# Sparse attention scores with a full-height rest of the keys, and block values in two 64-column products

## The chip, the cores and the metric

The program runs on one core of a Trainium2 chip, as one launch. The metric is the device time of one execution, in microseconds (us). TensorE multiplies matrices, VectorE and ScalarE work element by element, GpSimd (POOL) does some of that too, and SyncE (SP) issues most transfers between memory and the on-chip SBUF. TensorE writes only to PSUM, which is handed out here as two-bank tiles (`p2`, three of them) and one-bank tiles (`p1`, two of them).

## The reference, cut to what matters

Two transformer blocks on 512 tokens of 1024 features, in float32. The second block has two layers, each a mixer and a mixture of 16 experts. The mixer of its second layer is a sparse attention (`nsa_mixer`) with 16 heads of 64 features in 4 groups; the four heads of a group share keys and values. Each query is matched with three sets of keys, each with a softmax of its own, and the three results are added under gates:

```
p_cmp = masked_softmax(einsum('bghqd,bgcd->bghqc', qb, k_cmp), cmask)   # 31 compressed blocks
o_cmp = einsum('bghqc,bgcd->bghqd', p_cmp, v_cmp)
...                                                                     # the 16 best blocks of 64 keys
o_slc = einsum('bghqk,bgqkd->bghqd', p_slc, v_sel)
...                                                                     # the last 512 keys
o_win = einsum('bghqk,bgkd->bghqd', p_win, vw_b)
o = gb[..., 0:1] * o_cmp + gb[..., 1:2] * o_slc + gb[..., 2:3] * o_win
```

With 512 tokens there are 8 blocks, fewer than 16, and the window holds 512 keys, so both the selected and the window branch reach every earlier key under a causal mask. They differ in their keys and values.

## The kernel before, in words

Products that must be exact are done in rounded parts. A float32 matrix is split into a part rounded to the type `float32r` and the rest, and a product is the sum of rounded by rounded, rounded by rest and rest by rounded (`mm3`, L393 to L396, three matmuls into the same PSUM tile). Values and weights of the attention that stay plain float32 take two TensorE instructions for a product.

The attention works on token tiles of 128 queries, from the last tile (number 3) to the first, because the last sees the most keys: tile i sees n = 128(i+1) of them. Its steps, with their lines:

- `k_turn` (L1717) turns the keys of both branches feature-major, four token tiles one by one. The 64 features of each group stand twice, on rows 0 to 63 and 64 to 127. ScalarE rounds them into `kH` (L1725, two pages of SBUF, one for two groups); VectorE subtracts to get the rest into `kL` (L1728), one page: even groups on rows 0 to 63, odd groups on rows 64 to 127, so two subtractions of 64 rows for each pair of groups.
- The compressed keys `ck` (L1783 to L1790) hold the rounded part on all rows and beside it the rest, on the rows that meet the queries' rounded part, else zero. They have a small tile of their own. The compressed values `vbd` (L1797) are block-diagonal: for each group and each pair of heads a stationary matrix of 128 rows (4 heads of 32 block slots) by 128 columns (2 heads of 64 features).
- `q_parts` and `q_turn` (L1806, L1819) make the stacked queries `qT`: for a head, its rounded part on 64 rows and its rest on the other 64; which is on top depends on the group's parity.
- `weights` (L1869) does the scores of a head: for each branch one matmul of the stacked queries with `kH` (L1880, 128 rows, so both the rounded and the rest part of the queries), one of the queries' rounded part with `kL` (L1881, 64 rows), and one that adds the causal mask in bfloat16 (L1882, 128 columns). In the first two tiles, where 2n is at most 512, both branches go in one matmul each and two heads share a PSUM tile. VectorE then takes the row maximum (L1885), ScalarE the exponentials with their sums (L1889), VectorE scales by gate over sum (L1890 to L1894).
- `turn` (L1897) turns the weights with n/128 matmuls a branch and head (L1905), ScalarE copies them to SBUF (L1907).
- `values` (L1910) does a pair of heads: one product of `vbd` with the compressed weights, both heads at once (L1912, 128 columns, two instructions), then for each branch, key tile and head a product of 64 columns (L1916, two instructions each), the first head into rows 0 to 63 of the PSUM tile and the second into rows 64 to 127.

`csc` (L1836) and `compressed` (L1849) do the scores and weights on the compressed keys. The loop of L1942 runs over (tile, head); the scores run two heads ahead of the turns. When tile 1 begins, the output projection of tiles 2 and 3 (`project`, L1209) is mixed in three steps at a time, its matmuls being L394 to L396 with the name `op`. Behind the attention follow the projection of tiles 0 and 1, the routing, 16 experts and the last layer norm.

Two things set the order of work. The program is written in one order, and a planner with a simulated timeline (`schedule_with_timeline_sim`) then fixes each engine's instruction order at build time. And SBUF is handed out in 23 pages of four units by the class `Arena` (L209): `take` gives a request that needs a whole page the page that was freed longest ago, and `float32r` values and plain ones do not share a page. A tile on a reused page waits for the last reader of what was there. `kH0`, `kH1`, `kL` take three pages and are followed by the rounded and rest parts of the weights of the first key projection (`wh`, `wl`, L376).

Of the kernel before, what the change touches and what calls it, by code (L numbers as in the profile page):

```python
# [10 lines left out]
F32 = mybir.dt.float32  # L11
# [31 lines left out]
# ------------------------------------------------------------------ host side layout  # L43
# [164 lines left out]
# ------------------------------------------------------------------ device side  # L208
class Arena:  # L209
    """SBUF in pages of four units, handed out and taken back in the order of the program.  # L210

    A page holds either rounded values or plain ones; a free page that changes sides becomes a new tile."""
# [56 lines left out]
def build(ctx, tc, I, out, dbg=None):  # L269
# [36 lines left out]
    def load_a(name, dt=F32):  # L306
        """a constant in the arena, to be dropped after its last use"""
        ap = I[name]
        t = sb(ap.shape[1], name, dt)[:ap.shape[0]]
        nc.sync.dma_start(out=t, in_=ap)  # L310
        return t

    def after(i, name):
        """let an instruction go behind one that is needed sooner"""
        tc.add_manual_dep(i.ins, name, mybir.DependencyInfo(mybir.DependencyClass.NoSync, mybir.DependencyReason.SCHED_ONLY),
                          reason="what is needed sooner goes first")

    class Stream:
        """Weights in the order of their use, a page at a time; the ring's depth sets how far the loads run ahead."""
# [8 lines left out]
        def ahead(self, n):  # L328
            """request the next n pages here"""
# [11 lines left out]
        def later(self, ld):  # L341
            """queue a load behind those that are needed sooner"""
# [55 lines left out]
    def dense_fm(nk, x, cols, alloc=p2):  # L398
        """one 128-row output tile; x(k, sl) -> (H, L); cols: list of slices"""
# [7 lines left out]
    def tiles(n, w, tag, dt=F32):  # L407
        """n tiles of w columns, as many to a page as fit"""
# [17 lines left out]
    def newton(dst, xh, t):  # L426
        """a step towards 1/sqrt of one value per partition, of which xh holds minus a half, in two"""
# [5 lines left out]
    def rsq(dst, src, shape):  # L433
        """1/sqrt of a small positive tile, by Newton's steps from a guess on the bits"""
# [7 lines left out]
    # ---------------------------------------------------------------- load and split x  # L442
# [26 lines left out]
    def rstd_wide(dst, ps, cols, n):  # L469
        """1/sqrt(sum/n + eps) on every partition"""  # L470
# [17 lines left out]
    # ---------------------------------------------------------------- ssm: the transition and its powers  # L488
# [16 lines left out]
    def sincos(x, mul, nm):  # L505
        """sin and cos of mul*x, the argument brought to [-pi, pi]"""
# [20 lines left out]
    def cmul(ore, oim, ar_, ai, br, bi, ta, tb, eng, neg_im=False, conj=False):  # L527
        """(a)(b); conj: conj(a) b; neg_im: minus the imaginary part"""
# [56 lines left out]
    def big_cmul(o, fs, m0, xr, xi, neg_im, eng):  # L585
        """[pair, m, c] = lb^(m0+m) * x[pair, c]"""
# [40 lines left out]
    # rotation of the chunks' states  # L627
# [89 lines left out]
    # queries and gates fill the waits of the ssm; the gates are kept in memory until the mixing  # L717
# [45 lines left out]
    # ---------------------------------------------------------------- keys and values  # L763
# [52 lines left out]
    # ---------------------------------------------------------------- attention  # L816
# [21 lines left out]
    def att_out(osb, ss4, n, t0, skip=0):  # L838
        """sub-layer norm of n tokens of all heads, then transposed into the mixed tokens at t0"""
# [57 lines left out]
    # the mixer's own tail fills the waits of the attention  # L897
# [16 lines left out]
    def gated(m, ps):  # L914
        """(tanh + 1) * y, twice the sigmoid's product"""
# [71 lines left out]
    # ---------------------------------------------------------------- mixing, residual  # L987
# [34 lines left out]
    # ---------------------------------------------------------------- ffn  # L1022
# [25 lines left out]
    # ================================================================ second block  # L1048
# [14 lines left out]
    # the router's weights under the first layer norm of each layer: gain into the rows, the sums for mean and bias  # L1063
# [17 lines left out]
    # ---------------------------------------------------------------- gla in  # L1081
# [40 lines left out]
    def stream_tm(x, mid=None):  # L1122
        """token-major product, the weights streamed once; four [128, 512] accumulators; mid() goes in between"""
# [32 lines left out]
    # ---------------------------------------------------------------- layer norm, output projection, experts  # L1156
# [6 lines left out]
    def stats(bs, rs, mv):  # L1163
        """per token: 1/sqrt(var + eps), -mean/sqrt(var + eps), and the mean; of the sum over alpha; an operation a step"""
# [19 lines left out]
    def run(steps, n=None):  # L1184
        """the next n steps, or the rest of them"""
# [5 lines left out]
    class Layer:  # L1191
# [11 lines left out]
        def clear(self):  # L1203
            """rows of slots that no token takes"""
# [4 lines left out]
        def project(self, pair, free=()):  # L1209
            """two token tiles, in steps: the output projection, the weights streamed once for both, then the routing"""  # L1210
# [4 lines left out]
            def scores(nh):  # L1215
                """what half the features add to the router's scores"""
# [72 lines left out]
        def taken(self, pos, k, t):  # L1289
            """one-hot of the slots that tile t's tokens take with their choice k"""  # L1290
# [4 lines left out]
        def slots(self, q, idx):  # L1295
            """rows to gather and to scatter for each slot of each expert; empty slots fall out of bounds"""
# [5 lines left out]
        def route(self, ts):  # L1302
            """two tiles' choices, and their places among the tokens of each expert"""
            two, sc = slice(ts[0], ts[0] + 2), self.lgs[:, ts[0]:ts[0] + 2].rearrange("p t (g e) -> p (t g) e", e=4)
            # rows: the tokens' groups, then the groups' scores; each row twice, that a window of it reaches all others
# [527 lines left out]
    def half(g):  # L1833
        return slice(64 * (g % 2), 64 * (g % 2) + 64)
# [162 lines left out]
```

## Time and profile before

| | us |
|---|---|
| runs (3) | 1963.28, 1965.65, 1969.62; median 1965.65 |
| profiled execution, first to last instruction (span) | 1961.8 |
| median over span | 3.9 |
| TensorE busy | 1769.9 (90%) |
| VectorE busy | 1227.9 (63%) |
| ScalarE busy | 879.8 (45%) |

The profiled execution is told by its span; its own time outside the span is not on the page, so the median of the runs stands beside it. Times in the trace are counted from the start of the span. PE is TensorE's matmuls, PEld its weight loads, which run beside them; DVE is VectorE, ACT ScalarE. A matmul's duration reaches from its start to its modelled end and overlaps with the next one's, so the distance between two starts, not the duration, is what a matmul costs in a row of them. An instruction's tile is given as rows*columns of the stationary operand, then the result.

### The profile page before, as it was taken

What the parts mean: (1) busy time and instruction counts of PE and PEld (TensorE: products, weight loads), DVE (VectorE), ACT (ScalarE), POOL (GpSimd) and SP (SyncE); (2) the same over time, 40 slices, a digit from 0 to 9 for tenths busy, and PEclk for the clock granted to TensorE, in tenths of its full rate; (3) what the DMA queues carried; (4) which work ended last, traced back from release to release, by engine and by line L of the source; (5) the groups of instructions that cost most, each with busy time, mean ns of one, the idle gap of its engine ahead of it and who ended that gap; (6) DMA issues with size and microseconds to landing.
All of it is one profiled execution on the core that took longest, in us unless ns stands there. A gap on an engine that the chain in (4) does not pass through costs nothing. (4 is left out here: it accounts for less than half of the span.)

```text
span 1961.8 us, 27157 instructions
## 1 busy us (share of the span) xinstructions
PE 1769.9 (90%) x10655; PEld 1487.9 (76%) x10655; DVE 1227.9 (63%) x2264; ACT 879.8 (45%) x1396; POOL 222.0 (11%) x164
## 2 busy tenths in 40 slices
PE   8999999899999999989999599839999999959990
PEld 7899877798989988768887478738876777647870
DVE  7855468776555542343358699773337667558985
ACT  4233346433333322241224388733235666428881
POOL 2310000031000000000001222130000001022213
PEclk9999999899999999999999699969898999869995
DMA  5434222242322333212235499642420002538963
GB/s 190 126 100 132 82 87 70 73 169 79 106 86 89 105 124 107 105 64 87 86 126 218 138 343 381 241 162 92 132 68 16 12 1 99 199 141 308 377 241 137
DMA packets 69206, 269.73 MB, mean 137 GB/s; under 512 B 22144, under 2 KB 24720, under 8 KB 44240
## 3 DMA queue, kind: packets, MB, share of 16 engines
q1 hardware_dynamic: 52384, 246.38, 35.4%
q0 software_dynamic: 9216, 16.80, 2.3%
q10 hardware_dynamic: 7472, 4.76, 1.2%
q8 instruction: 85, 1.39, 0.3%
q14 instruction: 49, 0.40, 0.1%
HBM read 249.62 MB, written 30.43 MB: 143 GB/s over the span
## 5 line engine op out<-in xcount | busy, mean ns | idle before, releaser
L369 ACT CAST pg<-pg 128x1024 fp32r<-128x1024 f32 (+2 forms) x437 | 427.3, 1006 | 565.3 <-PE mm L395 219.4
L369 DVE TENSOR_TENSOR pg<-pg,pg 128x1024 fp32r<-128x1024 f32 (+2 forms) x437 | 506.5, 1183 | 276.0 <-ACT pg L369 261.4
L394 PE MATMUL mm<-pg,pg 128*128 128x258 f32 (+2 forms) x1504 | 484.9, 323 | 1.4 <-ACT pg L888 0.7
L396 PE MATMUL mm<-pg,pg 128*128 128x258 f32 (+2 forms) x1504 | 483.0, 322 | 3.0 <-DVE pg L369 3.0
L395 PE MATMUL mm<-pg,pg 128*128 128x258 f32 (+2 forms) x1504 | 482.6, 321 | 0.0
L394 PEld LDWEIGHTS mm<-pg,pg 128*128 128x128 f32 x1504 | 287.8, 192 | 27.8 <-ACT pg L886 2.7
L396 PEld LDWEIGHTS mm<-pg,pg 128*128 128x128 f32 x1504 | 286.7, 191 | 23.9 <-DVE pg L369 3.6
L395 PEld LDWEIGHTS mm<-pg,pg 128*128 128x128 f32 x1504 | 287.5, 191 | 21.2 <-issue 0.4
L360 DVE TENSOR_TENSOR pg<-mm,pg 128x256 f32<-128x256 f32 (+3 forms) x138 | 66.3, 511 | 139.7 <-PE mm L396 139.7
L360 POOL TENSOR_TENSOR pg<-pg,pg 128x1024 f32<-128x1024 f32 (+3 forms) x48 | 88.0, 1845 | 522.1 <-PE npt L1905 326.1
L395 PE MATMUL psh<-pg,pg 128*128 128x512 f32 x256 | 106.1, 414 | 2.3 <-DVE pg L369 2.3
L394 PE MATMUL psh<-pg,pg 128*128 128x512 f32 x256 | 101.4, 396 | 0.0
L396 PE MATMUL psh<-pg,pg 128*128 128x512 f32 x256 | 101.0, 395 | 0.0
L394 PE MATMUL tm<-pg,pg 128*128 128x512 f32 x192 | 76.4, 408 | 4.6 <-ACT pg L1145 4.6
L395 PE MATMUL tm<-pg,pg 128*128 128x512 f32 x192 | 77.2, 402 | 1.2 <-DVE pg L369 1.2
L396 PE MATMUL tm<-pg,pg 128*128 128x512 f32 x192 | 75.9, 396 | 0.0
L1885 DVE TENSOR_REDUCE nmx<-ns 128x2 f32<-128x1024 f32 (+3 forms) x48 | 50.2, 1045 | 39.0 <-PE ns L1882 38.7
L1889 ACT ACTIVATE pg<-ns,nmx 128x512 f32<-128x512 f32 (+3 forms) x128 | 66.2, 529 | 15.9 <-DVE nse L1890 5.8
L360 DVE TENSOR_TENSOR pg<-pg,pg 128x512 f32<-128x512 f32 (+12 forms) x100 | 55.2, 573 | 27.1 <-ACT pg L675 10.2
L1452 POOL DMA_INDIRECT yd<-pg,idx x32 | 42.0, 1314 | 162.3 <-ACT pg L1451 144.8
L360 DVE TENSOR_TENSOR pg<-pg 128x64 f32<-128x64 f32 (+9 forms) x126 | 48.1, 403 | 17.6 <-ACT pg L1033 15.4
L395 PEld LDWEIGHTS psh<-pg,pg 128*128 128x128 f32 x256 | 48.5, 190 | 13.2 <-DVE pg L369 4.4
(438 smaller groups left out, 2987.0 us busy)
## 6 DMA issues: line engine op xcount, KB each, us to landing
pg<-in_w_moe_dram SPq DMA_DIRECT2D x96, 1024.0 KB, 11.5
pg<-in_w_up_dram SPq DMA_DIRECT2D x22, 1024.0 KB, 4.9
pg<-in_w_dn_dram SPq DMA_DIRECT2D x11, 1024.0 KB, 4.8
pg<-in_w_g_dram SPq DMA_DIRECT2D x8, 1024.0 KB, 5.8
pg<-in_w_go_dram SPq DMA_DIRECT2D x8, 1024.0 KB, 5.1
pg<-yd SPq DMA_DIRECT2D x16, 512.0 KB, 6.0
pg<-in_w_n_dram SPq DMA_DIRECT2D x8, 1024.0 KB, 6.3
pg<-in_w_no_dram SPq DMA_DIRECT2D x8, 1024.0 KB, 5.0
```

The lines of the kernel that those rows point to most:

```text
L360: return (eng or V).tensor_tensor(o, a, b, op=op)
L369: return A.copy(h, src), V.tensor_tensor(l, src, h.bitcast(F32), op=ALU.subtract)
L394: TE.matmul(o, a[0], b[0], start=start, stop=False)
L395: TE.matmul(o, a[0], b[1], start=False, stop=False)
L396: TE.matmul(o, a[1], b[0], start=False, stop=stop)
L1452: s = G.indirect_dma_start(out=self.yd, out_offset=bass.IndirectOffsetOnAxis(ap=self.idx[:, 16 + e:17 + e], axis=0), in_=yo, in_offset=Non ...
L1885: V.tensor_reduce(mx, sc, axis=AX.X, op=ALU.max, negate=True)
L1889: A.activation(pp[:, r, br], sc[:, r, br], AF.Exp, bias=mx[:, r, br:br + 1], accum_out=se[:, r, br:br + 1])
```

## The change

The rest of the keys `kL` gets a page for each pair of groups, like `kH`, and holds the rest on all 128 rows; L1881 multiplies the whole stacked queries with it. Each of the four key pages is asked for with 2112 columns, a whole page, and its last 64 hold one group's compressed keys, so `ck` has no tile of its own. The product of the compressed values is done as two products of 64 columns, one for each head of the pair. Comments and docstrings go too, which moves a few line numbers and nothing else.

```diff
-    kH = [sb(2048, f"kH{a}", FR).rearrange("p (g b n) -> p g b n", g=2, b=2) for a in range(2)]
-    kL = sb(2048, "kL", FR).rearrange("p (g b n) -> p g b n", g=2, b=2)
+    kpg = [sb(2112, f"k{n}{a}", FR) for n in "HL" for a in range(2)]
+    kH, kL = ([t[:, :2048].rearrange("p (g b n) -> p g b n", g=2, b=2) for t in kpg[2 * i:2 * i + 2]] for i in range(2))
+
+    ck = [t[:, 2048:].rearrange("p (a c) -> p a c", c=32) for t in kpg]
...
             A.copy(kH[a][:, :, :, sl], src[:, 2 * a:2 * a + 2])
-            for r in range(2):
-                rows = slice(64 * r, 64 * r + 64)
-                tt(kL[rows, a, :, sl], src[rows, 2 * a + r], kH[a][rows, r, :, sl].bitcast(F32), ALU.subtract)
+            tt(kL[a][:, :, :, sl], src[:, 2 * a:2 * a + 2], kH[a][:, :, :, sl].bitcast(F32), ALU.subtract)
...
-    ck = sb(256, "ck", FR).rearrange("p (g a c) -> p g a c", g=4, c=32)
-    A.copy(ck[:, :, 0], kc[:, 0])
-    for r in range(2):
-        rows = slice(64 * r, 64 * r + 64)
-        tt(ck[rows, r::2, 1], kc[rows, 0, r::2], ck[rows, r::2, 0].bitcast(F32), ALU.subtract)
-        tt(ck[rows, 1 - r::2, 1], kc[rows, 0, 1 - r::2], kc[rows, 0, 1 - r::2], ALU.subtract)
+    for g in range(4):
+        A.copy(ck[g][:, 0], kc[:, 0, g])
+        for r in range(2):
+            rows = slice(64 * r, 64 * r + 64)
+            tt(ck[g][rows, 1], kc[rows, 0, g], ck[g][rows, 0].bitcast(F32) if r == g % 2 else kc[rows, 0, g], ALU.subtract)
...
-                      ck[:, 2 * hs + h // 4].rearrange("p a c -> p (a c)"), start=True, stop=True)
+                      ck[2 * hs + h // 4].rearrange("p a c -> p (a c)"), start=True, stop=True)
...
-                TE.matmul(o_, q[half(g)], kL[half(g), g // 2, br, :n], start=False, stop=False)
+                TE.matmul(o_, q, kL[g // 2][:, g % 2, br, :n], start=False, stop=False)
...
-        TE.matmul(o_, vbd[:, g, pr % 2].rearrange("p a d -> p (a d)"), pct[i][:, g * P:(g + 1) * P], start=True, stop=False)
+        for r in range(2):
+            TE.matmul(o_[64 * r:64 * r + 64], vbd[:, g, pr % 2, r], pct[i][:, g * P:(g + 1) * P], start=True, stop=False)
...
-    drop("kH0", "kH1", "kL", "ck", "vbd", "vsw", "qT", "qs", "rt", "pc", "pct", "pp", "pt")
+    drop("kH0", "kH1", "kL0", "kL1", "vbd", "vsw", "qT", "qs", "rt", "pc", "pct", "pp", "pt")
```

## Rows read from the trace of the kernel before

**Rows 1.** The chain of waits, 1480 to 1655 us, by line.

```profile
by line: PE npo L1916 21.3%; PE npt L1905 17.3%; PE ns L1881 16.7%; PE ns L1880 11.6%; PE ns L1882 7.1%; PE op L394 4.3%; PE op L396 4.2%; PE op L395 4.2%; PE csc L1842 3.2%; PE npo L1912 3.2%; PE qTp L1825 2.7%; PE lg L1227 1.0%; PE cpt L1
```

**Rows 2.** TensorE's waits, 1480 to 1655 us: total, times, longest.

```profile
PE ns L1880 <- DVE pg L1826: 1.1, 1, 1.1
PE ns L1880 <- ACT pg L1907: 0.5, 1, 0.5
```

**Rows 3.** Busy us by stretch: length, PE, PEld, DVE, ACT, POOL, clock, DMA, GB/s.

```profile
1480.00:1540.00 60.00, 58.87 (x449) 41.62 (x450) 41.55 (x89) 37.88 (x79) 0.00 (x0) 0.99 0.00 1
1540.00:1600.00 60.00, 59.55 (x464) 42.44 (x462) 40.71 (x100) 36.35 (x90) 0.00 (x0) 1.00 0.03 10
1600.00:1655.00 55.00, 55.00 (x372) 41.96 (x370) 38.71 (x96) 31.29 (x78) 0.00 (x0) 1.00 0.23 77
1655.00:1707.00 52.00, 48.51 (x298) 35.60 (x297) 30.81 (x105) 31.26 (x97) 10.72 (x7) 0.80 0.33 130
```

**Rows 4.** TensorE in order of time, tile 3: start us, us, instruction.

```profile
1527.17 0.48 PE L1880 MATMUL ns<-pg,pg 128*128 128x512 f32 x1
1527.58 0.49 PE L1881 MATMUL ns<-pg,pg 64*128 64x512 f32 x1
1528.00 0.23 PE L1882 MATMUL ns<-c_dmask,c_ident 128*128 128x128 bf16 x1
1528.07 1.04 PE L1905 MATMUL npt<-c_ident,pg 128*128 128x128 f32 x8
1529.04 0.43 PE L1916 MATMUL npo<-pg,pg 128*64 128x128 f32 x2
1529.40 0.50 PE L1880 MATMUL ns<-pg,pg 128*128 128x512 f32 x1
```

**Rows 5.** The same view where turns, projection and scores of tile 1 meet.

```profile
1612.35 1.03 PE L1905 MATMUL npt<-c_ident,pg 128*128 128x128 f32 x8
1613.14 0.48 PE L395 MATMUL op<-pg,pg 128*128 128x512 f32 x1
1613.46 0.39 PE L396 MATMUL op<-pg,pg 128*128 128x512 f32 x1
...
1613.92 0.39 PE L1880 MATMUL ns<-pg,pg 128*128 128x512 f32 x1
1614.24 0.50 PE L1881 MATMUL ns<-pg,pg 64*128 64x512 f32 x1
```

**Rows 6.** Weight loads by line, 1464 to 1710 us: busy, mean ns, idle before.

```profile
L1881 PEld LDWEIGHTS ns<-pg,pg 64*128 64x128 f32 x96 | 18.4, 191 | 21.2 <-issue 19.9
...
L1882 PEld LDWEIGHTS <-c_ident 128*128 128x128 bf16 x96 | 9.2, 96 | 20.6 <-issue 19.4
L395 PEld LDWEIGHTS op<-pg,pg 128*128 128x128 f32 x43 | 8.1, 189 | 1.4
```

**Rows 7.** The score tile's instructions: L1881 with its shapes.

```profile
L1881 PE MATMUL ns<-pg,pg x96: 379/492/792, 1464.9 to 1694.3; 64*128 64x512 f32 x48, 64*128 64x384 f32 x32, 64*128 64x256 f32 x16
```

**Rows 8.** TensorE in order of time, tile 2, 384 columns.

```profile
1543.07 0.43 PE L1881 MATMUL ns<-pg,pg 64*128 64x384 f32 x1
1543.44 0.23 PE L1882 MATMUL ns<-c_dmask,c_ident 128*128 128x128 bf16 x1
```

**Rows 9.** The same view, tile 3: a compressed-value product, and a row of value products.

```profile
1525.22 0.44 PE L1912 MATMUL npo<-pg,pg 128*128 128x128 f32 x2
1525.49 1.04 PE L1905 MATMUL npt<-c_ident,pg 128*128 128x128 f32 x8
...
1531.30 1.96 PE L1916 MATMUL npo<-pg,pg 128*64 128x128 f32 x30
```

**Rows 10.** The turned keys' tile: its subtractions (ns), and who waited for it.

```profile
L360 DVE TENSOR_TENSOR pg<-kTp,pg x16: 353/422/428, 1391.1 to 1399.2; 64x256 fp32r<-64x256 f32 x16
...
  PE kTp L1721: 3.4, 1
```

**Rows 11.** ScalarE: the rounding of the second weight pair of the key projection.

```profile
1332.30 1.05 ACT L369 CAST pg<-pg 128x1024 fp32r<-128x1024 f32 x1 [1.13 <-POOL pg L360]
```

More of the change, by code (lines that the diff above doesn't have):

```diff
@@ L1831, in pairs_tm @@
         return x
-    def half(g):
-        return slice(64 * (g % 2), 64 * (g % 2) + 64)
     def csc(i, hs):
```

## The prediction

> **What bounds the kernel now.** I read the chain of waits first, then the table by stage, then the instructions of one head in order of time. The change lies in the sparse attention of the second block's second layer, some 245 of 1961.8 us. The chain between 1480 and 1655 us [rows 1] is TensorE almost throughout: the value products, the turns of the weights, the score products (L1880, L1881, L1882). TensorE's own waits in those 175 us come to 1.6 us [rows 2]; by stage it is busy for 58.9 of 60, 59.6 of 60 and 55 of 55 us, VectorE for 41.6, 40.7 and 38.7, ScalarE for 37.9, 36.4 and 31.3 [rows 3]. So up to 1655 us TensorE sets the pace and the others have three to four tenths of their time free. In the last token tile (1655 to 1707) the granted clock is 0.80 on the mean, TensorE is busy for 48.5 of 52 us and short chains through the other two engines decide as well.
>
> Busy time says nothing of a matmul's price, since matmuls overlap; start-to-start times do. In the steady state [rows 4] L1880 (128 rows, 512 columns) is followed by L1881 (64 rows, 512 columns) after 0.41 us, that by the mask product L1882 after 0.42 us, and that by the next work after 0.07 us. The projection's matmuls, also 512 columns wide but all with 128 rows [rows 5], run differently: the first after a row of turns takes 0.32 us (1613.14 to 1613.46), the next two together 0.46 us, 0.23 each. Where L1880 follows one of these, L1881 still comes only 0.32 us later (1613.92 to 1614.24). So going from 128 to 64 rows costs 0.09 us and coming back 0.42 - 0.23 = 0.19 us. The weight loads say the same [rows 6]: the 96 loads of L1881 leave 21.2 us idle before them and the 96 of L1882 20.6 us, nearly all with no releaser in the profile, whereas 43 loads of L395, all rows, have 1.4 us.
>
> **The change, part by part.**
>
> *The rest of the keys on 128 rows.* L1881 becomes as tall as its neighbours; columns and count stay. There are 48 groups of 512 columns, 32 of 384 and 16 of 256 [rows 7]. A group of 512 goes from 0.41 + 0.42 to 0.32 + 0.23 us: 0.28 saved, 48 x 0.28 = 13.4 us. With 384 columns the way back is 0.37 us [rows 8]; a full-row product of that width must lie between one weight load (0.189 us, rows 6) and 0.23 us. I take 0.20, so 0.17 + 0.09 = 0.26 us saved, 32 x 0.26 = 8.3 us. For 256 columns I bound the saving by 0 and 0.28 us and take 0.15, as the shorter product hides less of its load: 2.4 us. The first two tiles' 21.7 us is all TensorE time. How much reaches the end depends on what is next: with some 20 us less, VectorE's 121 busy us [rows 3] fall on 155 us instead of 175, 78% against 69%, ScalarE's 105.5 us are 68%. Neither is full, but VectorE's row-maximum and ScalarE's exponentials come in bursts, so some of TensorE's hidden waits will show: I count 92%, 20 us. The short last tile lets half of its 2.4 us through: 1.2 us. Ends for the whole part: 0 (if the intervals have another cause) and 25.4 us (96 groups, 0.28 for each but the last 16, and 0.15 to 0.28 for these).
>
> Here a rule speaks against the change. The rows say that full-row loads run under the matmul ahead of them (L395's loads, 1.4 us idle in 43). The Trainium skill ("TensorE: Matmul & The Clock Gate", Part 3, The mechanism) says that weight loads overlap with matmuls in flight only when the row group differs; by that rule 128 rows after 128 rows would overlap no better than 64 after 128, and this part would be worth nothing. The trace disagrees for full-row pairs, so I go by the rows, and the rule is a rival below.
>
> *Compressed values as two 64-column products.* Two instructions of L1912 (a float32 product takes two) become four of 64 columns. Between a mask product and turns the two now take 0.27 us (1525.22 to 1525.49) [rows 9]; thirty 64-column instructions of L1916 take 1.96 us, 0.065 each, so four take 0.26. Placed right ahead of L1916 the part is worth nothing either way, because the passage to 64 columns is paid there anyhow. Placed alone among full-width work it pays a passage of its own: turns followed by L1916 take 0.97 us (1528.07 to 1529.04) [rows 4] against 0.79 us followed by full-width work (1612.35 to 1613.14) [rows 5], 0.18 in; L1916's two instructions then occupy 0.36 us (1529.04 to 1529.40) instead of 0.13, 0.23 out. Alone, a pair so costs 0.18 + 0.23 + 0.26 - 0.27 = 0.40 us more. There are 32 pairs, so the ends are 0 and 12.8 us. Both placings occur in the trace; I take half alone, 6.4 us, and 6 us of it on the path.
>
> The Trainium skill ("TensorEngine Tiling (Array Packing)", Key Properties) has a change of tiling mode drain the array, which is a charge on this part alone wherever its products stand between others. Charged at the rows' 0.41 us a round trip the sum stays as it is.
>
> *Splitting the keys.* Sixteen 64-row subtractions of 256 columns, 0.422 us each [rows 10], become eight of 128 rows and 512 columns. Bounds: as long as the half-row one (8 x 0.422, saving 3.4 us) or twice that (saving 0). I take 1.3 us saved on VectorE; TensorE waits 3.4 us for these subtractions [rows 10], so 1 us reaches the end.
>
> *Compressed keys in the tails of the four key pages.* One ScalarE copy and four VectorE subtractions become four and eight smaller ones. None is in the trace; between 0 and a full 0.422 us each the seven more cost 0 to 3 us. They lie under the query projection, whose matmuls keep TensorE busy for tens of microseconds before the scores need these keys. I take 0; without that cover it would be up to 3 us.
>
> *Pages.* kL grows from one page to two and ck gives its unit back. The arena gives out the pages that were freed longest ago, so the pages behind kL move by one: the first pair of rounded projection weights gets the page of the layer norm's gain and bias, which in the trace is free only when GpSimd is done, just before 1332.3 us [rows 11]. The earlier pair now loses its head start, and with it a subtraction that today stands ahead of VectorE's statistics. I bound this by 2 us both ways and take 0.
>
> Sum: -20 - 1.2 + 6 - 1 = -16.2; rounded with the arena's and planner's unknowns to -17 us. On the profiled execution that is a span of 1961.8 - 17 = 1944.8 us. The runs lie 1.5 to 7.8 us above that span, their median 1965.65 is 3.9 above it, so the median becomes 1948.6 us. The experts behind the attention start from what it hands them and their weights are asked for as it frees pages, so I shift all behind it by the same amount.
>
> **Rivals.**
>
> (B) *The load, not the rows.* If a full-row load waits for the matmul ahead as the half-row one does, the score part is worth nothing and the value part costs its 6 us less 1 us of key splitting: 1965.65 + 5 = 1970.7 us, or 1965 where the value products stand with L1916. Against it: L395's loads [rows 6] and the 0.23 us of rows 5. For it: only the projection's rows show full-row pairs at 0.23 us, none of the score products do. This is what the Trainium skill's rule quoted above would give.
>
> (C) *VectorE and ScalarE become the bound.* If their bursts take half of the 20 us, the gain is 10 + 1.2 + 1 - 6 = 6 us: 1959 us; with the value products cheap, 1954. For it: the exponential waits for the maximum, which waits for L1882. Against it: 69% and 60% busy [rows 3].
>
> (D) *The two 64-column products stand apart.* The order on TensorE is written ahead by a planner. If it sets the first and the second of a pair into different gaps, each pays 0.41 us of passage beside 0.13 us of work: 2 x 0.54 - 0.27 = 0.81 us more a pair, 26 us for 32. This outweighs the 20 + 1.2 + 1 = 22 us gained as soon as the mean is above 0.69 us a pair: 1965.65 + 26 - 22 = 1969.7 us, and up to 1972 where VectorE also holds some of the 22 back. For it: the planner already tears a single call of L1916 off its row [rows 4]. Against it: that call waits for different data, the two new ones are ready together.
>
> **How the numbers follow.** My forecast has 0.66, C 0.18, B 0.08, D 0.08. The forecast's own range is 1938 to 1957: the lower end is 25.4 us of scores, 1 us of splitting and 1 us of pages, no loss in values, the upper 8.5 us of net gain. C reaches to 1960. From 1938 to 1961 I leave out B and D, 16 in 100, and little else. About 0.3%, 5.9 us, is what a measurement of this kernel can tell from no change; below 1959.8 lie the forecast and nearly all of C (0.82), within 5.9 us the rest of C and the lower halves of B and D (0.11), above 1971.5 their upper halves (0.07).
>
> **What would show it.** Right: L1880 to L1881 at about 0.32 us, L1881 to L1882 at 0.23 (0.20 for 384 columns), and the idle time ahead of the loads of L1881 and L1882 down from 41.8 us to under 5. The attention's stretch shorter by 15 to 20 us and everything behind it in step. Values: four 64-column instructions in a row at 0.065 us; alone, with 0.18 and 0.23 us around them. C shows as waits of TensorE for the turns' and values' operands well above 1.6 us. Wrong would be: intervals as before (B), single pairs of 64-column instructions amid full-width work (D), or a first key projection that waits for its weights.

## The result, and the profile after

| | before | after |
|---|---|---|
| runs, median (us) | 1967.63 (1963.28 to 1969.64, 4 runs) | 1942.47 (1940.47 to 1945.68, 4 runs) |
| span of the profiled execution (us) | 1961.8 | 1939.5 |
| sparse attention, first score product to last value product (us) | 241.5 | 222.0 |
| all that follows it (us) | 255.7 | 257.2 |

The ratio is 0.9888 [0.9868, 0.9909]: 22 us by the ratio, 25 by the medians, where 17 were forecast. Lines have moved by up to 4: L1880, L1881 and L1882 of before (score products) are L1876, L1877 and L1878, L1905 (turns) is L1901, L1912 and L1916 (values) are L1909 and L1913.

The span is 22.3 us shorter, and the trace splits this by the first and last matmul of each stage: 1.3 us ahead of the layer's first projection, where the code is the same (chance: two executions of one and the same kernel, no_height below, differ by 4.1 us there); 1.2 us in that projection (37.8 to 36.6); 1.8 us from there to the first score product (125.0 to 123.2); 19.5 us in the attention; and 1.5 us given back behind it.

The chain of waits, 1475 to 1633 us, which answers to [rows 1]. TensorE is still nearly all of it; L1877's share has gone from 16.7% to 9.0%:

```profile
by line: PE npo L1913 21.7%; PE npt L1901 20.0%; PE ns L1876 12.3%; PE ns L1877 9.0%; PE op L394 4.9%; PE op L395 4.8%; PE npo L1909 4.8%; PE op L396 4.7%; PE ns L1878 3.5%; PE qTp L1824 3.3%; PE csc L1838 2.6%; DVE nmx L1881 1.6%; ACT pg L
```

TensorE in order of time (start us, duration, instruction), which answers to [rows 4, 8]: a group of 512 columns, one of 384, one of 256.

```profile
1515.58 0.48 PE L1876 MATMUL ns<-pg,pg 128*128 128x512 f32 x1
1515.89 0.40 PE L1877 MATMUL ns<-pg,pg 128*128 128x512 f32 x1
1516.13 0.23 PE L1878 MATMUL ns<-c_dmask,c_ident 128*128 128x128 bf16 x1
...
1538.92 0.42 PE L1876 MATMUL ns<-pg,pg 128*128 128x384 f32 x1
1539.18 0.33 PE L1877 MATMUL ns<-pg,pg 128*128 128x384 f32 x1
1539.35 0.23 PE L1878 MATMUL ns<-c_dmask,c_ident 128*128 128x128 bf16 x1
...
1669.11 0.37 PE L1876 MATMUL ns<-pg,pg 128*128 128x256 f32 x1
1669.31 0.28 PE L1877 MATMUL ns<-pg,pg 128*128 128x256 f32 x1
1669.43 0.28 PE L1878 MATMUL ns<-c_dmask,c_ident 128*128 128x256 bf16 x1
```

From start to start the two passages now take 0.31 + 0.24 us where [rows 4] had 0.41 + 0.42, 0.26 + 0.17 with 384 columns, and 0.20 + 0.12 with 256. The last pair has no row ahead of the prediction; in the kernel before it is, at full clock, 0.29 + 0.31:

```profile
1690.89 0.36 PE L1880 MATMUL ns<-pg,pg 128*128 128x256 f32 x1
1691.18 0.38 PE L1881 MATMUL ns<-pg,pg 64*128 64x256 f32 x1
1691.49 0.28 PE L1882 MATMUL ns<-c_dmask,c_ident 128*128 128x256 bf16 x1
```

So the saving is 0.28 us a group at 512 and at 256 columns alike: a fixed price of two changes of height, not a share of the product's length. The medians over all groups at full clock say the same: the two passages together take 0.84, 0.72 and 0.61 us before (512, 384 and 256 columns) and 0.55, 0.44 and 0.32 us after.

Weight loads by line, 1460 to 1690 us (busy us, mean ns, idle us before), which answer to [rows 6]:

```profile
L1877 PEld LDWEIGHTS ns<-pg,pg 128*128 128x128 f32 x96 | 19.2, 200 | 0.1
L1878 PEld LDWEIGHTS <-c_ident 128*128 128x128 bf16 x96 | 9.4, 98 | 19.8 <-issue 19.1
L395 PEld LDWEIGHTS op<-pg,pg 128*128 128x128 f32 x46 | 9.0, 197 | 1.8 <-DVE pg L369 0.2
```

The idle time ahead of L1877's loads fell from 21.2 us to 0.1, that ahead of the mask's loads stayed at 19.8 (20.6 before). I had read the second number as part of the price. It is none: L1877 to L1878 became 0.18 us shorter with the same idle time ahead of the mask's loads. The time at which a load starts tells more. Before, the load of the half-height product starts with its own matmul (L1881 at 1527.58 us in [rows 4]); now it starts and ends under the matmul ahead (L1876, from 1515.58 to 1516.06 us):

```profile
1527.58 0.18 PEld L1881 LDWEIGHTS ns<-pg,pg 64*128 64x128 f32 x1 [0.24 <-issue]
```

```profile
1515.66 0.19 PEld L1877 LDWEIGHTS ns<-pg,pg 128*128 128x128 f32 x1
```

TensorE's waits, 1475 to 1633 us (total, times, longest), and the busy time by stretch (length, PE, PEld, DVE, ACT, POOL, granted clock, DMA share, GB/s; the last stretch is the last token tile), which answer to [rows 2, 3]:

```profile
PE ns L1876 <- DVE pg L1825: 0.8, 1, 0.8
PE ns L1876 <- ACT pg L1903: 0.5, 1, 0.5
PE npt L1901 <- DVE pg L360: 0.4, 1, 0.4
```

```profile
1476.00:1532.00 56.00, 55.03 (x494) 41.38 (x492) 42.39 (x94) 38.83 (x83) 0.00 (x0) 0.99 0.00 1
1532.00:1584.00 52.00, 51.46 (x464) 39.28 (x462) 39.44 (x96) 36.06 (x89) 0.00 (x0) 1.00 0.04 12
1584.00:1633.00 49.00, 48.56 (x331) 37.76 (x330) 35.10 (x77) 28.92 (x71) 0.00 (x0) 1.00 0.25 85
1633.00:1685.00 52.00, 44.29 (x354) 34.24 (x353) 38.39 (x121) 32.71 (x103) 9.63 (x7) 0.90 0.40 150
```

In the first three tiles TensorE still waits for next to nothing (1.7 us; 1.6 before), with VectorE at 75% and ScalarE at 66%. In the last tile it is idle for 7.7 of 52 us, for 3.5 before, mostly for ScalarE's exponentials (waits of L1901, 1633 to 1685 us; the first row was 1.2 us before):

```profile
PE npt L1901 <- ACT pg L1885: 4.2, 4, 1.9
PE npo L1909 <- ACT pg L1862: 1.1, 1, 1.1
PE npt L1901 <- DVE pg L1890: 0.8, 1, 0.8
```

Two small parts. The turned keys' tile has eight subtractions at 0.680 us where [rows 10] had sixteen at 0.422, and TensorE's wait for it is 2.3 us instead of 3.4. ScalarE's rounding of the key projection's weights [rows 11] now handles both in one go from 1329.86 us, ahead of the time at which the second alone had started:

```profile
L360 DVE TENSOR_TENSOR pg<-kTp,pg x8: 627/680/692, 1388.7 to 1394.4; 128x512 fp32r<-128x512 f32 x8
...
  PE kTp L1723: 2.3, 1
```

```profile
1329.86 2.00 ACT L369 CAST pg<-pg 128x1024 fp32r<-128x1024 f32 x2 [2.25 <-DVE pg L369]
```

What the change costs is in TensorE's instructions in order of time. Here the planner has put the two compressed products of one pair into different gaps:

```profile
1531.07 1.09 PE L1901 MATMUL npt<-c_ident,pg 128*128 128x128 f32 x8
1532.10 0.43 PE L1909 MATMUL npo<-pg,pg 128*64 128x128 f32 x2
1532.46 0.44 PE L1876 MATMUL ns<-pg,pg 128*128 128x384 f32 x1
...
1533.39 0.23 PE L1878 MATMUL ns<-c_dmask,c_ident 128*128 128x128 bf16 x1
1533.55 0.43 PE L1909 MATMUL npo<-pg,pg 128*64 128x128 f32 x2
1533.92 0.33 PE L1901 MATMUL npt<-c_ident,pg 128*128 128x128 f32 x1
```

Ahead of it the turns take 1.03 us, where they take 0.79 ahead of full-width work [rows 5]; then its two instructions take 0.36. Counted over the attention, runs of 64-column products with full-width work on either side ("stretches" below) went from 47 to 64; 19 of the 64 hold compressed products alone, six of them half a pair.

### The profile page after: what moved, and what is told of

It reads as the page before. It is cut to its first block, busy times and chain, and to the rows that moved or that the text cites. A ratio compares the mean times of both kernels' runs of the same rounds, so it can differ in the third digit from the quotient of the medians.

```text
span 1939.5 us, 27284 instructions
## 1 busy us (share of the span) xinstructions
PE 1747.8 (90%) x10719; PEld 1480.7 (76%) x10719; DVE 1227.6 (63%) x2260; ACT 879.2 (45%) x1399; POOL 220.9 (11%) x164
## 5 line engine op out<-in xcount | busy, mean ns | idle before, releaser
L396 PE MATMUL mm<-pg,pg 128*128 128x258 f32 (+2 forms) x1504 | 482.6, 322 | 4.3 <-DVE pg L369 4.3
L394 PE MATMUL mm<-pg,pg 128*128 128x258 f32 (+2 forms) x1504 | 484.4, 322 | 1.6 <-ACT pg L888 0.7
L394 PEld LDWEIGHTS mm<-pg,pg 128*128 128x128 f32 x1504 | 287.3, 191 | 28.0 <-ACT pg L886 2.9
L396 PEld LDWEIGHTS mm<-pg,pg 128*128 128x128 f32 x1504 | 286.2, 190 | 25.3 <-DVE pg L369 5.1
L395 PEld LDWEIGHTS mm<-pg,pg 128*128 128x128 f32 x1504 | 286.9, 191 | 21.2 <-issue 0.4
L394 PE MATMUL psh<-pg,pg 128*128 128x512 f32 x256 | 102.0, 399 | 0.0
L396 PE MATMUL psh<-pg,pg 128*128 128x512 f32 x256 | 101.4, 396 | 0.0
L394 PE MATMUL tm<-pg,pg 128*128 128x512 f32 x192 | 76.3, 408 | 4.5 <-ACT pg L1145 4.5
L396 PE MATMUL tm<-pg,pg 128*128 128x512 f32 x192 | 75.9, 395 | 0.0
L1881 DVE TENSOR_REDUCE nmx<-ns 128x2 f32<-128x1024 f32 (+3 forms) x48 | 50.0, 1043 | 19.7 <-PE ns L1878 19.4
```

Source lines behind the costliest of these rows:

```text
L394: TE.matmul(o, a[0], b[0], start=start, stop=False)
L395: TE.matmul(o, a[0], b[1], start=False, stop=False)
L396: TE.matmul(o, a[1], b[0], start=False, stop=stop)
L1881: V.tensor_reduce(mx, sc, axis=AX.X, op=ALU.max, negate=True)
```

## The experiments

Theory: a product on 64 rows among products on 128 pays 0.28 us a group, so the height of L1877 is the gain; each stretch of 64-column products pays about 0.41 us for the way in and out, so the split of the values costs 17 x 0.41 = 7 us. Rivals: the order and the pages that come with the change make the gain, and stretches cost nothing because TensorE has time to spare.

What varies most from one execution to the next is the clock that TensorE is granted (1.0 is its level of 2.4 GHz, 0.5 that of 1.2; a mean between them is a mixture). So for each profile this table has the length of the attention, the mean granted clock of just that stretch, and their product, which stands for its length at full clock (an estimate; the clock's two decimals leave 1.2 us of doubt, and the five executions with a height of 64 and 47 stretches lie between 224.5 and 227.0). The last column does the same for the whole program: the time of each run multiplied by the mean granted clock of that run, averaged over the runs; for the kernel before it is 1854 to 1855 us on the three chips used.

| kernel | height | stretches | length (us) | clock | product (us) | ratio of the runs to before | runs, time x clock (us) |
|---|---|---|---|---|---|---|---|
| before | 64 | 47 | 241.5 | 0.94 | 227.0 | 1 | 1854 to 1855 |
| page_only | 64 | 47 | 238.8 | 0.94 | 224.5 | 0.9987 [0.9974, 1.0000] | 1850 |
| tails_only | 64 | 47 | 237.3 | 0.95 | 225.4 | 0.9955 [0.9938, 0.9972] | 1855 |
| no_height | 64 | 47 | 235.9 | 0.96 | 226.5 | 0.9946 [0.9927, 0.9964] | 1855 |
| no_height_again | 64 | 47 | 235.9 | 0.96 | 226.5 | 0.9958 [0.9941, 0.9976] | 1854 |
| values_only | 64 | 67 | 250.4 | 0.92 | 230.4 | 0.9987 [0.9971, 1.0003] | 1860 |
| values_again | 64 | 67 | 238.3 | 0.97 | 231.2 | 0.9991 [0.9975, 1.0007] | 1860 |
| after | 128 | 64 | 222.0 | 0.95 | 210.9 | 0.9888 [0.9868, 0.9909] | 1837 |
| after_again | 128 | 64 | 222.4 | 0.96 | 213.5 | 0.9874 [0.9851, 0.9896] | 1839 |
| keys_only | 128 | 47 | 213.5 | 0.97 | 207.1 | 0.9854 [0.9831, 0.9878] | 1832 |
| one_row_last | 128 | 32 | 212.4 | 0.95 | 201.8 | 0.9808 [0.9788, 0.9828] | 1828 |
| late_head_first | 128 | 32 | 209.7 | 0.97 | 203.4 | 0.9804 [0.9783, 0.9825] | 1828 |

Four rows of this table as the trace has them, by the view of busy time (columns as above):

keys_only:

```profile
1458.00:1671.50 213.50, 199.94 (x1610) 156.69 (x1610) 163.94 (x430) 142.85 (x359) 10.50 (x7) 0.97 0.17 63
```

no_height:

```profile
1456.70:1692.60 235.90, 227.40 (x1611) 163.66 (x1610) 164.64 (x430) 143.74 (x359) 10.49 (x7) 0.96 0.16 57
```

values_only, with 5 us from the start of the attention:

```profile
1467.70:1718.10 250.40, 242.62 (x1675) 170.88 (x1674) 164.56 (x430) 144.09 (x359) 10.48 (x7) 0.92 0.14 50
...
1492.00:1497.00 5.00, 5.00 (x15) 2.90 (x15) 2.34 (x5) 2.36 (x6) 0.00 (x0) 0.50 0.00 0
```

values_again, the same kernel, with two such pieces:

```profile
1464.70:1703.00 238.30, 230.97 (x1674) 162.84 (x1674) 164.42 (x430) 144.12 (x359) 10.49 (x7) 0.97 0.15 52
...
1469.00:1474.00 5.00, 1.92 (x8) 1.52 (x8) 5.00 (x22) 3.57 (x11) 0.00 (x0) 0.75 0.60 211
1489.00:1494.00 5.00, 5.00 (x65) 4.32 (x66) 3.68 (x10) 3.76 (x10) 0.00 (x0) 1.00 0.02 3
```

**keys_only**: the keys' part of the change alone, shown against the kernel after.

```diff
-        for r in range(2):
-            TE.matmul(o_[64 * r:64 * r + 64], vbd[:, g, pr % 2, r], pct[i][:, g * P:(g + 1) * P], start=True, stop=False)
+        TE.matmul(o_, vbd[:, g, pr % 2].rearrange("p a d -> p (a d)"), pct[i][:, g * P:(g + 1) * P], start=True, stop=False)
```

> The keys' part of the change alone: rest of the keys on 128 rows, splitting, pages; the compressed values again as one product of 128 columns. Theory (each passage of TensorE between full-width and 64-column products costs 0.41 us a round trip, and the two-product form adds round trips): the planned order has 47 stretches of 64-column products against 64 in the changed kernel, so 17 x 0.41 = 7 us less than the changed kernel: ratio to before 0.985, about 1938 us where before is 1967.6. Rival (the two-product form is free or pays): 0.989 or more, as the changed kernel.

Measured: 1936.69 us against 1963.65, 0.9854. The theory's value. It lies below the whole change's 0.9888, as it should where the split of the values costs, but the two intervals overlap, so these times alone do not show it.

**no_height**: as keys_only, but the score product with the rest reads 64 rows of the new pages.

```diff
-                TE.matmul(o_, q, kL[g // 2][:, g % 2, br, :n], start=False, stop=False)
+                TE.matmul(o_, q[64 * (g % 2):64 * (g % 2) + 64], kL[g // 2][64 * (g % 2):64 * (g % 2) + 64, g % 2, br, :n], start=False, stop=False)
```

> Everything of the keys' part but the row height: four key pages, rest of the keys split and stored on 128 rows, but the score product reads only 64 of them as before; compressed values as one product of 128 columns. Left out against the changed kernel: the product of the queries' rest with the keys' rest. Theory (the row height is what pays, 0.28 us a group): only the pages (2.4 us) and the splitting (1.8 us) remain, ratio 0.998, about 1963.4 us; idle ahead of the half-height loads again about 41 us. Rival (pages and shorter splitting carry the gain, or heights of 64 and 128 rows cost the same): 0.985 to 0.990.

Measured: 1953.07 us, 0.9946. Without the height the intervals are the old ones, 0.41 and 0.42 us:

```profile
1518.35 0.48 PE L1876 MATMUL ns<-pg,pg 128*128 128x512 f32 x1
1518.76 0.49 PE L1877 MATMUL ns<-pg,pg 64*128 64x512 f32 x1
1519.18 0.23 PE L1878 MATMUL ns<-c_dmask,c_ident 128*128 128x128 bf16 x1
```

From here to keys_only it is 0.0092 of the time, 18 us, for the height alone (20 us from no_height_again below; 22 to 23 us by the table's last column). In the two traces the instructions of TensorE, VectorE and ScalarE stand in the same order up to the last value product, so that no change of the planner's comes in between. TensorE's busy time falls by 227.40 - 199.94 = 27.5 us (96 groups at 0.28 are 26.9; some 3 us of the fall go with the clock, 0.97 instead of 0.96); the attention shortens by 22.4 us, 19.4 of them at equal clock. The 5 us between 27.5 and 22.4 are new waits, 13.6 us instead of 8.5. The miss is that no_height itself gained some 6 us more than expected.

A rival that I had not named: L1877 now has the same stationary operand as L1876, the stacked queries, and that could be what makes it cheap. It can't make most of the saving. 0.19 of the 0.28 us lie between L1877 and the mask product, which have different operands, and L396, L394 and L1880 in [rows 5], each with another operand on 128 rows, follow one another after 0.23 us.

**page_only**: the kernel before with one page more taken behind `kL`, unused.

```diff
+    sb(2048, "kX", FR)
     o = stream_tm(x4a)
+    drop("kX")
```

> The kernel before with one more page taken behind the keys' pages and given back after the first key projection, nothing else. Theory (the first pair of rounded projection weights moves to a later page, so its subtraction no longer stands ahead of VectorE's statistics of the last token tile): the key projection starts 2.4 us earlier, 1337.3 us instead of 1339.7, and the end with it: ratio 0.9988. Rival (the earlier start comes from somewhere else in the change): start at 1339.7 us as before, ratio 1.000.

Measured: 1961.26 us, 0.9987 [0.9974, 1.0000]. As the theory had it, and too little for no_height's 10.6 us. The key projection starts at 1337.5 us. What brings it forward is in the projection just ahead of it, the layer's first: there TensorE's idle time falls from 5.9 us to 3.3 (37.80 - 31.89 and 36.50 - 33.16), and it is 3.2 to 3.4 us in every kernel here with the four pages:

```profile
1301.80:1339.60 37.80, 31.89 (x216) 31.44 (x217) 25.82 (x43) 15.73 (x34) 15.45 (x6) 0.88 0.15 47
```

```profile
1300.90:1337.40 36.50, 33.16 (x216) 32.69 (x217) 25.08 (x43) 15.40 (x34) 15.39 (x6) 0.83 0.13 45
```

**tails_only** and **no_height_again**: the second is no_height once more; the first takes the split subtractions out of it and keeps the four pages with the compressed keys in their tails.

```diff
-            tt(kL[a][:, :, :, sl], src[:, 2 * a:2 * a + 2], kH[a][:, :, :, sl].bitcast(F32), ALU.subtract)
+            for r in range(2):
+                rows = slice(64 * r, 64 * r + 64)
+                tt(kL[0][rows, a, :, sl], src[rows, 2 * a + r], kH[a][rows, r, :, sl].bitcast(F32), ALU.subtract)
...
-                TE.matmul(o_, q[64 * (g % 2):64 * (g % 2) + 64], kL[g // 2][64 * (g % 2):64 * (g % 2) + 64, g % 2, br, :n], start=False, stop=False)
+                TE.matmul(o_, q[64 * (g % 2):64 * (g % 2) + 64], kL[0][64 * (g % 2):64 * (g % 2) + 64, g // 2, br, :n], start=False, stop=False)
```

> The kernel before with four key pages and the compressed keys in their tails, but the rest of the keys still in one of these pages, by sixteen 64-row subtractions, and read on 64 rows; the fourth page holds only its tail of compressed keys. Open is why the half-height version with the split keys gained 10.6 us (0.9946) where pages and splitting were worth 4 to 5. If the pages and the tails make the rest: about 0.995. If it is the split subtractions, or scatter of that timing: 0.9985 to 0.9988, as with the one extra page alone (page move 2.4 us at the first key projection, nothing else).

> The half-height version with split keys once more: the whole keys' part of the change, but the score product with the rest of the keys reads 64 rows only, and the compressed values are one 128-column product. If its first timing (0.9946 [0.9927, 0.9964]) holds: 0.993 to 0.996. If that was scatter and only the page move and the split subtractions count (2.4 + 1.8 us): about 0.998.

Measured: 1957.60 us, 0.9955, and 1956.12 us, 0.9958. So no_height's gain was no scatter, and splitting the subtractions adds nothing that can be told. By the times the pages with their tails bring 9 us [5.5, 12]. Where is only partly found: tails_only's profiled execution is 4.4 us shorter than that of before, 1.4 of it in the layer's first projection and 4.2 in the attention, 1.6 there at equal clock. The planned order does not tell it from page_only: TensorE's instructions stand in the same order in both traces up to the last value product, and the profiled executions are 1957.4 and 1957.9 us long.

What differs over the runs is the granted clock, on the mean 0.947 in tails_only, 0.949 and 0.947 in the two timings of no_height, but 0.943 in page_only and 0.943 to 0.944 in the runs of before beside them. With the clock taken out (the table's last column) tails_only and no_height are where before is, and page_only is 4 to 5 us below it. That column corrects too much, since in the runs of one kernel the time falls by only some two thirds of what the clock rises (a fit over all runs); corrected by two thirds, these kernels are all 3 to 4 us below before. So at most 4 us can be put down to the pages, 2.6 of them where page_only has them; the rest of the 9 us goes with the clock, and why that is higher in some kernels is open.

**values_only** and **values_again**: the kernel before with the compressed product split in two, twice.

```diff
-        TE.matmul(o_, vbd[:, g, pr % 2].rearrange("p a d -> p (a d)"), pct[i][:, g * P:(g + 1) * P], start=True, stop=False)
+        for r in range(2):
+            TE.matmul(o_[64 * r:64 * r + 64], vbd[:, g, pr % 2, r], pct[i][:, g * P:(g + 1) * P], start=True, stop=False)
```

> The two 64-column products alone on the kernel before. Theory: the planned order has 67 stretches of 64-column products against 47, 20 x 0.41 = 8 us slower, less what the other engines' waits hide: ratio 1.003 to 1.004, 1973 to 1976 us. Rival (they sit with the other 64-column products and are free): 1.000. Second rival (they save a passage in each pair, 32 x 0.2 us): 0.997.

> The kernel before with the compressed value product split into two of 64 columns, nothing else, once more: its first timing gave 0.9987 [0.9971, 1.0003] where 1.003 to 1.004 was expected, and its profiled execution had a stretch of the attention at a granted clock near 0.6. Theory (20 more stretches at 0.41 us each, on a TensorE that has the same waits as before): 1.002 to 1.004, and an attention of 241.5 + 6 to 8 = 248 to 250 us in an execution whose clock is that of the kernel before. Rival (in the kernel before the passages fall into time in which TensorE waits anyway, or the planner's other order gives them back): 0.997 to 1.000 and an attention of about 241 us.

Measured: 1962.08 and 1962.26 us, 0.9987 and 0.9991. By the times the theory failed here twice: 20 more stretches and no loss. The profiles say why in part. At equal clock the attention is 230.4 and 231.2 us long against 227.0 (226.5 in no_height), 4 us more, 0.2 us a stretch; TensorE's busy time times the clock is 223 to 224 us against 218. But the length itself was 250.4 us in one execution and 238.3 in the other, with the clock at 0.92 and 0.97: 12 us between two executions of one kernel, three times the effect. In both, the clock fell to 0.50 after TensorE had waited at the start of the attention (in values_again it was busy for 1.92 of 5 us at 1469 us); in values_again it was back at 1.00 in the stretch from 1489 us, in values_only still at 0.50 in that from 1492, with TensorE busy throughout. The clock over all runs fits the profiles: on the mean 0.947 in both timings, against 0.944 and 0.943 in the runs of before beside them. With the clock taken out, the split costs 5 to 6 us (the table's last column; 3 us corrected by two thirds). So the stretches do cost, and in the times a higher clock hid it; why the clock was higher is open.

**one_row_last**, **late_head_first** and **after_again**: if stretches cost, their number can be brought down to one a pair and tile, 32. A stretch is torn where its first product has its data and the next has not; giving the later head's product first, and the compressed products last, leaves nothing that could start early. one_row_last against the kernel after:

```diff
-        for r in range(2):
-            TE.matmul(o_[64 * r:64 * r + 64], vbd[:, g, pr % 2, r], pct[i][:, g * P:(g + 1) * P], start=True, stop=False)
         for br in range(2):
             for c in range(i + 1):
-                for r in range(2):
+                for r in (1, 0):
                     TE.matmul(o_[64 * r:64 * r + 64], vsw[:, c * 512 + br * 256 + g * 64:c * 512 + br * 256 + (g + 1) * 64],
-                              pts[r][:, br, c * P:(c + 1) * P], start=False, stop=br == 1 and c == i)
+                              pts[r][:, br, c * P:(c + 1) * P], start=br == 0 and c == 0, stop=False)
+        for r in (1, 0):
+            TE.matmul(o_[64 * r:64 * r + 64], vbd[:, g, pr % 2, r], pct[i][:, g * P:(g + 1) * P], start=False, stop=True)
```

late_head_first against keys_only:

```diff
-                for r in range(2):
+                for r in (1, 0):
```

> The changed kernel, with the order inside values() turned: of each chunk the later head's product is given first, and the two compressed products come last and close the sum. Theory (each separate stretch of 64-column products costs TensorE one passage in and one out, together about 0.41 us by the start-to-start times of the trace after, and the changed kernel has 64 such stretches where one per pair and tile is enough): 32 stretches, 32 fewer than the changed kernel, so 32 x 0.41 = 13 us less than it, about 0.982 of the kernel before, and the attention from the first score product to the last value product 222 - 13 = 209 us. Rival (the stretches cost nothing end to end, because TensorE waits there for the planes of weights anyway; the changed kernel's distance from the kernel with the keys' part alone is scatter): as the changed kernel and the keys' part alone, 0.985 to 0.989. Rival on the other side (to begin with the later head's product makes the whole group wait for the later plane, and work that filled that wait is gone): above 0.990.

> The keys' part of the change alone (compressed values as one 128-column product, as before), with the later head's product given first within each chunk, so that no 64-column product starts before both heads' planes of weights are there: 32 stretches of 64-column products where the keys' part alone has 47. Theory: 15 x 0.41 = 6 us less than the keys' part alone, 0.9854 - 0.003 = about 0.982 of the kernel before, and equal to the changed kernel with its order turned (both have 32 stretches). Rival (stretches cost nothing): 0.985, as the keys' part alone. Rival on the other side (the group waits longer as a whole): above 0.988.

> The changed kernel once more, beside the other kernels of this comparison on one chip. Theory (17 more stretches of 64-column products than the keys' part alone, at 0.41 us): about 0.988 to 0.989 of the kernel before, so 0.003 above the keys' part alone. Rival (the split of the compressed product costs nothing, as the split alone on the kernel before showed with 0.9987): 0.985 to 0.986.

Measured: 1929.18, 1927.30 and 1941.21 us against 1966.31: 0.9808, 0.9804, 0.9874. The theory's order and nearly its sizes: 12 us between 64 and 32 stretches on the same chip (13 expected), and the intervals of 32 and of 64 stretches do not touch. Of the 12 us, 10 lie in the attention, which is 212.4 us long where 209 had been expected, and 2.5 behind it. Between keys_only and late_head_first, timed on different chips, it is some 9 us by the times (6 expected) and 4 with the clock taken out. Their profiled executions, of which keys_only's is its fastest run, are equally long (1927.9 and 1928.0 us), though late_head_first's attention is 3.8 us shorter. With the row in one piece the split of the compressed product is free, as one_row_last and late_head_first are equal. TensorE in one_row_last, where L1911 and L1914 are the values and the compressed values:

```profile
1519.96 0.23 PE L1878 MATMUL ns<-c_dmask,c_ident 128*128 128x128 bf16 x1
1520.12 1.97 PE L1911 MATMUL npo<-pg,pg 128*64 128x128 f32 x32
1521.92 0.39 PE L1914 MATMUL npo<-pg,pg 128*64 128x128 f32 x4
1522.24 0.66 PE L1860 MATMUL cpt<-c_ident,pg 128*128 128x128 f32 x4
```

All 36 instructions of the pair stand together, 2.12 us. The waits that the turned order brings are small: TensorE waits 1.8 us over the attention for the later weights (L1903):

```profile
PE npt L1901 <- ACT pg L1885: 4.4, 3, 3.5
...
PE npo L1911 <- ACT pg L1903: 1.8, 5, 0.7
```

At equal clock the table gives 0.22 us a stretch (half height, 47 to 67), 0.30 (keys_only to the mean of the two executions of after), 0.32 (these to one_row_last) and 0.25 (keys_only to late_head_first): below the 0.41 us that I had from one pair alone.

These two kernels beat both the one before and the one after.

## Why the prediction was right, point by point

- *Height of the rest.* The mechanism was right and its size near: 24.1 us of TensorE time forecast, 27 measured (96 groups at 0.28 us), since 256 columns save 0.28 us like 512 and not 0.15. The floor that I had set for the narrower products, a full-row weight load of 0.189 us, does not hold: L1877 to L1878 takes 0.17 us with 384 columns and 0.12 with 256. The load that belongs to that passage is the mask's, 0.096 us [rows 6]. (My upper end, 25.4 us, is not the sum that I gave for it, which comes to 24.8 to 26.9.) Of the part 21.2 us were to reach the end; 18 to 20 did by the times, 22 at equal clock. In the last tile 16 x 0.28 = 4.5 us were saved and TensorE's waits, mostly for the exponentials, grew by 4.2. One sign failed: 19.9 us of idle time stayed ahead of the two lines' loads, where I had forecast under 5.
- *Rival B* falls. The Trainium skill's rule ("TensorE: Matmul & The Clock Gate", Part 3, The mechanism), that loads overlap with matmuls in flight only when the row group differs, does not hold for the loads of L1877: on 128 rows, they run under a matmul on 128 rows (the load at 1515.66 us), with 0.1 us idle ahead of 96, against 21.2 us on 64 rows.
- *Compressed values.* 6 us forecast; 4 to 7 by the runs (keys_only against the two timings of after, with intervals that overlap), 5 in the attention at equal clock, and 5 to 6 for the split alone with the clock taken out. The way to it was the one forecast: half of the 32 pairs alone, and in the trace 19 stretches of compressed products alone, 17 stretches more in all; the price of one is nearer 0.3 us than 0.40. The drain on a change of tiling mode, which the Trainium skill has in "TensorEngine Tiling (Array Packing)", Key Properties, agrees with one_row_last's 12 us. I had charged it to this part alone, but the runs show a like price, 0.28 us, for the change of height that the other part takes away.
- *Rival D* happened to some pairs (the rows at 1532.10 and 1533.55 us; six stretches of half a pair), not to all, and cost far less than its 26 us. *Rival C* happened in the last tile alone, where TensorE's idle time grew by 4.2 us; up to there VectorE and ScalarE had room.
- *Splitting the keys*: 1 us forecast. The eight subtractions together are 5.4 us, less than the 6.8 of the sixteen, as taken; no time of the runs can tell it.
- *Pages and compressed keys in the tails*: taken as 0, bounded by 2 and 3 us. This is the mis-sized term: tails_only is 9 us faster by the times, of which at most 4 remain at equal clock. 2.6 us of that stand at the place that I had named, as idle time of TensorE ahead of the key projection.
- *The clock* had no term. Put together, the runs give by the times -9 for pages and tails, -19 for the height and +5 for the values, -23 us, where the sum was -21.2 + 6 - 1 and 0. At equal clock (the estimate above, with the whole or two thirds of the clock's difference taken out) the changed kernel is 15 to 20 us below before, on both sides of the forecast's 17. So the mechanism and the sum held, and the rest of the measured 22 to 25 us goes with a granted clock that was higher in the runs of after_again than in those of before (0.947 against 0.943). No part of the prediction foresaw that, and that it came out as a gain is luck as far as is known.

## What to carry to other kernels

What a matmul costs beside its neighbours is a matter of their shape: before trimming a product to half of the rows or columns, read the start-to-start times on both sides of it, as a full-height product can be cheaper than two changes of height, even where half of it is not needed. Where odd shapes are needed, keep them in one piece, and give first the one whose data comes last. An edit costed at nothing deserves a run of its own. And where kernels differ by less than a per cent, their times are to be read beside the granted clock of the same runs: here 0.4% of clock looked like a gain of the pages and hid a cost of the values.

## What the runs showed that I had not expected

- The price of a change of height does not depend on the columns (0.28 us for the way there and back at 512 and at 256).
- Idle time ahead of weight loads is no price by itself: the mask's loads kept 19.8 us of it while the product ahead of them became 0.18 us cheaper.
- Two profiled executions of one kernel had a granted clock of 0.92 and 0.97 over the attention and differed by 12 us there; what made the clock come back later in one of them is not known.
- The mean granted clock over all runs differed between kernels, 0.943 to 0.949, and was repeated when a kernel was timed again on another chip (no_height 0.949 and 0.947, the split values 0.947 twice, before 0.943 to 0.944 three times).
